# Cross entropy on one core: the first 64 rows split into groups of 16 and 48

## The chip, the core and the metric

The kernel runs on one NeuronCore of a Trainium2 chip. The metric is the device time of one execution in microseconds. Times of a kernel are medians over several runs; the profile is one more execution, taken with the hardware profiler.

## What is computed

For each of 256 rows of 32,000 float32 logits the result is minus the log probability of the row's label:

```
log_probs = logits - np.max(logits, axis=-1, keepdims=True)
log_probs = log_probs - np.log(np.sum(np.exp(log_probs), axis=-1, keepdims=True))
return np.array([-log_probs[i, labels[i]] for i in range(batch)])
```

The kernel leaves the maximum out (the logits are standard normal draws) and computes, for a row x with label l, the logarithm of sum_j exp(x_j) times exp(-x_l). That is the same number. The input is 256 x 32,000 x 4 bytes = 32.77 MB, each byte is read once, and the output is 1 KB.

## The kernel before

**Groups and loads.** The rows are cut into groups of 64, 128, 32 and 32. A group of k rows is spread over all 128 partitions: each row takes q = 128/k neighbouring partitions, and each partition holds 32,000/q consecutive elements of one row (the list `flat`). A group is loaded in pieces of columns:

```
GROUPS = [64, 128, 32, 32]
LOADS = [
    [1024, 14976],
    [8896, 8192, 8320, 6592],
    [4736, 3264],
    [2496, 1824, 1344, 992, 736, 608],
]
```

The numbers are elements per partition, so the 14 loads have the numbers 0 to 13. Load 0 takes the first 1,024 elements of each partition's 16,000, load 1 the other 14,976. For a partition, every load is one consecutive run in DRAM; from one partition to the next, in loads 0 and 1, the run moves on by 16,000 x 4 = 64,000 bytes.

**Slots.** Loads 0 to 5 have a buffer each (slots 0 to 5). Load 6 reuses slot 2, load 7 slot 3, and loads 8 to 13 lie side by side in slot 1 as `x_tail`. The slot sizes are multiples of 64 elements, and slot 0 begins with 32 unused elements (`SKIP`), so that with the 128 bytes of constants ahead of them every slot's data begin at a multiple of 256 bytes in the partition. In loads 0 to 8 the runs in DRAM also begin at multiples of 256 bytes from the tensor's start, and are multiples of 256 bytes long. From load 9 on, sizes such as 1,824 elements are odd multiples of 128 bytes, and some of the runs begin, in DRAM and in the slot alike, 128 bytes past a multiple of 256.

**Order.** All loads are issued by SyncE (SP, line 206) in order of number. The first is moved ahead of the barrier at the program's start (`begin_first_load_before_barrier`); loads 1 to 5 follow at once. Load 6 is issued when VectorE is done with the data of load 2, load 7 when it is done with those of load 3, and the six loads of the tail after these; the last of them, load 13, shares a semaphore with load 5 and waits until that has landed.

**Steps.** `step(i)` works on load i. ScalarE (ACT) takes the exponential of the whole piece in place (line 215). For loads 0, 1, 12 and 13 ScalarE also sums along the row of the partition as it goes (`accum_out`). For loads 2 to 11 (`HALVED`) VectorE (DVE) adds the two halves of the piece and sums the result (line 294). TensorE multiplies the 128 partial sums by a 128 x k matrix `weights` (line 300), which adds up the partitions of a row in PSUM. For the first group, the two sums of loads 0 and 1 are added by a VectorE reduction (line 284) and multiplied once (line 285). The logarithm is taken by ScalarE (line 222): for the first group between the exponentials of loads 2 and 3, for the others at the end. A store from SP (line 318) ends the program. Sixteen matmuls without use (line 291) come before the last products.

**The weights.** `weights` is 0 where a partition doesn't belong to a row, and exp(-x_l) of the row where it does. Its 0/1 pattern `holds` is made by GpSimd (POOL) with two selections for each group (lines 261 and 265). The labels arrive by a DMA from ScalarE's queue (line 229), are spread over the partitions, and lead two indirect DMAs of GpSimd (line 250) to the 256 label logits `g_at`. At the end of step 1 (`GATHERED`) ScalarE takes their exponential (line 274), VectorE makes two diagonal matrices (line 276), TensorE spreads them (line 279), and VectorE multiplies by `holds` (line 282).

Of the kernel before, what the change touches and what calls it, by code (L numbers as in the profile page):

```python
# [2 lines left out]

# [6 lines left out]
P = 128  # L10
ROWS = 2
F32 = mybir.dt.float32
I32 = mybir.dt.int32
AF = mybir.ActivationFunctionType

GROUPS = [64, 128, 32, 32]

LOADS = [  # L20
    [1024, 14976],
    [8896, 8192, 8320, 6592],
    [4736, 3264],
    [2496, 1824, 1344, 992, 736, 608],
]
CHUNKS = [n for ns in LOADS for n in ns]
GROUP_OF = [g for g, ns in enumerate(LOADS) for _ in ns]

# [10 lines left out]
GATHERED = 1  # L39

HALVED = range(2, 12)
# [75 lines left out]
def kernel(  # L117
# [6 lines left out]
    nc = tc.nc  # L124
    nc.at_finalize(begin_first_load_before_barrier)
    nc.at_finalize(end_before_store_lands)
    B, C = logits.shape
    assert B == P * ROWS == sum(GROUPS)
    row_at = [sum(GROUPS[:g]) for g in range(len(GROUPS) + 1)]
    for k, ns in zip(GROUPS, LOADS):  # L130
        assert P % k == 0 and sum(ns) * P == k * C
    assert C % (P // min(GROUPS)) == 0


    flat = [
        logits[row_at[g]:row_at[g + 1], :].rearrange("k (q c) -> (k q) c", q=P // k)
        for g, k in enumerate(GROUPS)
    ]
    starts = [sum(ns[:j]) for ns in LOADS for j in range(len(ns))]
    first_of = [GROUP_OF.index(g) for g in range(len(GROUPS))]  # L140
    last_of = [first_of[g] + len(ns) - 1 for g, ns in enumerate(LOADS)]
    last = len(CHUNKS) - 1

    big = ctx.enter_context(tc.tile_pool(name="big", bufs=1))
    small = ctx.enter_context(tc.tile_pool(name="small", bufs=1))
    psum = ctx.enter_context(tc.tile_pool(name="psum", bufs=1, space=bass.MemoryType.PSUM))

    width = {}
    for i, s in enumerate(SLOTS):
        width[s] = max(width.get(s, 0), CHUNKS[i])  # L150
    width[TAIL_SLOT] = max(width[TAIL_SLOT], sum(CHUNKS[TAIL:]))


    place = []
    for i, s in enumerate(SLOTS):
        skip = SKIP if s == 0 else 0
        t = big.tile([P, skip + width[s]], F32, name=f"x{i}", tag=f"slot{s}")
        place.append(t[:, skip:skip + CHUNKS[i]])
    assert all(width[s] % 64 == 0 for s in width)
    tail = big.tile([P, width[TAIL_SLOT]], F32, name="x_tail", tag=f"slot{TAIL_SLOT}")  # L160
    for i in range(TAIL, last + 1):
        at = sum(CHUNKS[TAIL:i])
        place.append(tail[:, at:at + CHUNKS[i]])


    assert HALVED[0] == last_of[0] + 1 and HALVED[-1] == last - 2
    assert all(CHUNKS[i] % 2 == 0 for i in HALVED)
    parts = small.tile([P, len(LOADS[0])], F32, name="parts")
    row_0 = small.tile([P, 1], F32, name="row_0")
    near = {i: small.tile([P, 1], F32, name=f"near{i}") for i in range(HALVED[0], last + 1)}  # L170
    res = small.tile([1, B], F32, name="res")
    ident = small.tile([P, P], F32, name="ident")
    ones = small.tile([P, P], F32, name="ones")
    diag = [small.tile([P, P], F32, name=f"diag{r}") for r in range(ROWS)]

    holds = small.tile([P, B], F32, name="holds")
    weights = small.tile([P, B], F32, name="weights")


    bank = [psum.tile([P, 512], F32, name=f"bank{b}") for b in range(5)]  # L180
    lane = []
    for g, k in enumerate(GROUPS):
        b = 0 if g == 0 else 2 if g == len(GROUPS) - 1 else 1
        at = row_at[g] if b == 1 else 0
        lane.append(bank[b][0:1, at:at + k])
    mid = bank[1][0:1, row_at[1]:row_at[-2]]
    spread = bank[3][:, 0:B]

    warm, lbl_up = bank[4][0:1, 0:P], bank[4][:, 0:ROWS]
# [14 lines left out]
    def load(i):  # L204
        a = starts[i]
        nc.sync.dma_start(out=place[i], in_=flat[GROUP_OF[i]][:, a:a + CHUNKS[i]])  # L206

    def exps(i):
        if i in HALVED:
            acc = None  # L210
        elif i > last_of[0]:
            acc = near[i][:, :]
        else:
            acc = parts[:, i:i + 1]
        nc.scalar.activation(out=place[i], in_=place[i], func=AF.Exp, accum_out=acc)  # L215

    def weigh(g):

        return weights[:, row_at[g]:row_at[g + 1]]

    def logs(rows, sums):
        nc.scalar.activation(out=res[0:1, rows], in_=sums, func=AF.Ln)  # L222

    with tc.manual_schedule():
        first = len(set(SLOTS))
        for i in range(first):
            load(i)

        nc.scalar.dma_start(
            out=words[:, :], in_=bass.AP(tensor=lbl_words, offset=0, ap=[[2 * B, 1], [1, 2 * B]])  # L230
        )


        assert C <= 1 << 24
        nc.vector.memset(one[:, :], 1.0)
        nc.vector.memset(ones[:, :], 1.0)
        nc.vector.tensor_copy(out=lbl_row[:, :], in_=words[:, 0:2 * B:2])  # L237
        for r in range(ROWS):
            nc.tensor.matmul(  # L239
                lbl_up[:, r:r + 1], lbl_row[:, r * P:(r + 1) * P], one[:, :], start=True, stop=True  # L240
            )
        nc.vector.tensor_copy(out=lbl[:, :], in_=lbl_up)  # L242
        for r in range(ROWS):
            nc.gpsimd.iota(
                out=idx[:, r:r + 1], pattern=[[1, 1]], base=r * P * C, channel_multiplier=C
            )
        make_identity(nc, ident[:, :])
        nc.gpsimd.tensor_add(out=idx[:, :], in0=idx[:, :], in1=lbl[:, :])
        for r in range(ROWS):
            nc.gpsimd.indirect_dma_start(  # L250
                out=g_at[:, r:r + 1],
                out_offset=None,
                in_=logits[:, :],
                in_offset=bass.IndirectOffsetOnAxis(ap=idx[:, r:r + 1], axis=1),
            )
        nc.gpsimd.memset(holds[:, :], 1.0)
        for g, k in enumerate(GROUPS):
            q = P // k
            h = holds[:, row_at[g]:row_at[g + 1]]

            nc.gpsimd.affine_select(  # L261
                out=h, in_=h, pattern=[[-q, k]], base=0, channel_multiplier=1,
                compare_op=mybir.AluOpType.is_ge, fill=0.0,
            )
            nc.gpsimd.affine_select(  # L265
                out=h, in_=h, pattern=[[q, k]], base=q - 1, channel_multiplier=-1,
                compare_op=mybir.AluOpType.is_ge, fill=0.0,
            )

        def step(i):  # L270
            exps(i)
            g = GROUP_OF[i]
            if i == GATHERED:
                nc.scalar.activation(out=eg[:, :], in_=g_at[:, :], func=AF.Exp, scale=-1.0)  # L274
                for r in range(ROWS):
                    nc.vector.tensor_scalar_mul(diag[r][:, :], ident[:, :], eg[:, r:r + 1])  # L276

                for r in range(ROWS):
                    nc.tensor.matmul(  # L279
                        spread[:, r * P:(r + 1) * P], ones[:, :], diag[r][:, :], start=True, stop=True  # L280
                    )
                nc.vector.tensor_mul(out=weights[:, :], in0=holds[:, :], in1=spread)  # L282
            if i == last_of[0]:
                nc.vector.reduce_sum(out=row_0[:, :], in_=parts[:, :], axis=mybir.AxisListType.X)
                nc.tensor.matmul(lane[0], row_0[:, :], weigh(0), start=True, stop=True)
            if i == last_of[0] + 1:
                logs(slice(0, row_at[1]), lane[0])
            if i == WARM_FROM:
                col = place[i][:, CHUNKS[i] - 1:CHUNKS[i]]
                for _ in range(WARM):  # L290
                    nc.tensor.matmul(warm, col, diag[0][:, :], start=True, stop=True)  # L291
            if i in HALVED:
                half = CHUNKS[i] // 2
                nc.vector.scalar_tensor_tensor(  # L294
                    out=place[i][:, 0:half], in0=place[i][:, 0:half], scalar=1.0,
                    in1=place[i][:, half:CHUNKS[i]],
                    op0=mybir.AluOpType.mult, op1=mybir.AluOpType.add, accum_out=near[i][:, :],
                )
            if g:
                nc.tensor.matmul(  # L300
                    lane[g], near[i][:, :], weigh(g), start=i == first_of[g], stop=i == last_of[g]
                )


        assert GATHERED <= last_of[0]
        done = 0
        for i in range(first, last + 1):
            slot = SLOTS[i] if i < TAIL else TAIL_SLOT
            while done <= SLOTS[:first].index(slot):
                step(done)  # L310
                done += 1
            load(i)
        for i in range(done, last + 1):
            step(i)

        logs(slice(row_at[1], row_at[-2]), mid)
        logs(slice(row_at[-2], B), lane[-1])
        nc.sync.dma_start(
            out=out.rearrange("(a n) -> a n", a=2), in_=res[0:1, :].rearrange("o (a n) -> o a n", a=2)
        )  # L320
# [30 lines left out]
```

## Time and profile before

| | before |
|---|---|
| median of 5 runs | 83.41 us (82.5 to 84.42) |
| the profiled execution's own time | 82.56 us |
| its span, first to last instruction | 80.9 us |
| ScalarE busy | 57.4 us, 71% |
| VectorE busy | 27.6 us, 34% |
| TensorE busy | 11.0 us, 14% |
| GpSimd busy | 5.2 us, 6% |
| read from HBM | 32.77 MB, 405 GB/s over the span |
| granted TensorE clock | 1.00 |

The share of busy time is a mean over stages. Where a stage waits is read from the idle time ahead of an instruction and what ended it. The execution with the profiler took 82.56 us, of which 80.9 us are span and 1.66 us lie around it; it is near the fastest of the five other runs.

### The profile page before, as it was taken

The page shows a single profiled execution, that of the slowest core. Times are in us where ns is not written, and L with a number is a line of the kernel's source. Part 1 is how long each engine was busy: PE and PEld are TensorE (multiplying, and loading weights), DVE is VectorE, ACT ScalarE, POOL GpSimd, SP SyncE. Part 2 cuts the span into 40 slices and gives each one's busy share as a digit, 9 for nine tenths or more (in the row PEclk, how much of TensorE's full clock was granted, in tenths as well). Part 3 has the DMA queues.
Part 4 walks back from the last instruction along what each step waited for, and adds up shares of the span by engine and source line. Part 5 has one row for each costly group of instructions (what it writes and reads, how often), then busy time and mean ns, then how long its engine had stood idle before and what let it go on. Part 6 is the DMA issues. An engine that isn't in the chain of part 4 may idle for free.

```text
span 80.9 us, 261 instructions
## 1 busy us (share of the span) xinstructions
PE 11.0 (14%) x66; PEld 6.2 (8%) x66; DVE 27.6 (34%) x28; ACT 57.4 (71%) x23; POOL 5.2 (6%) x20
## 2 busy tenths in 40 slices
PE   0130000000000000061000020020000201159931
PEld 0130000000000000040000000000000000036710
DVE  1100000000000000030039908930099198898870
ACT  6230000000499999999999991599979999999993
POOL 4038810000000000000000000000000000000000
PEclk9999999999999999999999999999999999999999
DMA  4999999579969799899898997999899999999930
GB/s 119 614 474 474 474 444 415 237 326 474 545 299 563 317 528 389 389 518 405 372 526 362 428 510 319 456 456 469 379 440 412 409 419 420 430 416 409 417 146 1
DMA packets 2084, 32.77 MB, mean 405 GB/s; under 512 B 290, under 2 KB 291, under 8 KB 1060
## 3 DMA queue, kind: packets, MB, share of 16 engines
q1 hardware_dynamic: 2018, 32.77, 94.9%
q0 software_dynamic: 64, 0.00, 0.1%
q10 hardware_dynamic: 2, 0.00, 0.0%
HBM read 32.77 MB, written 0.00 MB: 405 GB/s over the span
## 4 chain that ended last, share of the span: by engine, by line
DMA 61%; ACT 34%; SPq 1%; another core or an unknown queue 1%; issue 1%; PE 0%
DMA x<-in_logits_dram 61%; ACT x L215 24%; ACT x_tail L215 9%; SPq L206 1%; PE bank L300 0%; ACT res L222 0%
## 5 line engine op out<-in xcount | busy, mean ns | idle before, releaser
L215 ACT ACTIVATE x<-x 128x1024 f32<-128x1024 f32 (+7 forms) x8 | 48.1, 6030 | 21.4 <-DMA x<-in_logits_dram 21.4
L294 DVE SCALAR_TENSOR_TENSOR x<-x 128x4448 f32<-128x4448 f32 (+5 forms) x6 | 21.8, 3631 | 15.3 <-ACT x L215 15.3
L276 DVE TENSOR_SCALAR diag<-ident,eg 128x128 f32<-128x128 f32 x2 | 0.5, 284 | 29.4 <-ACT eg L274 29.4
L300 PE MATMUL bank<-weights,near 128*1 128x32 f32 (+1 forms) x24 | 3.7, 263 | 34.1 <-DVE x L294 32.3
L215 ACT ACTIVATE x_tail<-x_tail 128x2496 f32<-128x2496 f32 (+5 forms) x6 | 7.5, 1302 | 0.0
L279 PE MATMUL bank<-diag,ones 128*128 128x128 f32 x4 | 1.2, 461 | 30.0 <-DVE diag L276 30.0
L291 PE MATMUL bank<-diag,x 128*1 128x128 f32 x32 | 5.0, 333 | 0.0
L294 DVE SCALAR_TENSOR_TENSOR x_tail<-x_tail 128x1248 f32<-128x1248 f32 (+3 forms) x4 | 4.1, 1025 | 0.6 <-ACT x_tail L215 0.3
L300 PEld LDWEIGHTS bank<-weights,near 128*1 128x1 f32 x24 | 1.0, 82 | 36.8 <-DVE x L294 34.6
L291 PEld LDWEIGHTS bank<-diag,x 128*1 128x1 f32 x32 | 3.2, 102 | 1.6
L279 PEld LDWEIGHTS bank<-diag,ones 128*128 128x128 f32 x4 | 0.9, 324 | 30.1 <-DVE diag L276 30.1
L250 POOL DMA_INDIRECT g_at<-in_logits_dram,idx x2 | 2.1, 1031 | 0.6 <-issue 0.3
L198 ACT ACT_TABLE_LOAD x1 | 1.3, 1283 | 0.8 <-PEq L335 0.8
L239 PE MATMUL bank<-one,lbl_row 1*128 1x1 f32 x4 | 1.0, 352 | 3.8 <-DVE lbl_row L237 3.8
L239 PEld LDWEIGHTS bank<-one,lbl_row 1*128 1x128 f32 x4 | 0.9, 317 | 3.8 <-DVE lbl_row L237 3.8
L237 DVE CAST lbl_row<-words 1x256 f32<-1x256 int32 x1 | 0.3, 282 | 2.3 <-DMA words<-in_labels_dram 2.3
L265 POOL TENSOR_SCALAR_AFFINE_SELECT holds<-holds 128x32 f32<-128x32 f32 (+2 forms) x4 | 1.0, 238 | 0.3
L261 POOL TENSOR_SCALAR_AFFINE_SELECT holds<-holds 128x32 f32<-128x32 f32 (+2 forms) x4 | 1.0, 238 | 0.1
L282 DVE TENSOR_TENSOR weights<-holds,bank 128x256 f32<-128x256 f32 x1 | 0.4, 422 | 1.2 <-PE bank L279 1.2
L222 ACT ACTIVATE res<-bank 1x64 f32<-1x64 f32 (+2 forms) x3 | 0.7, 219 | 0.1
L242 DVE CAST lbl<-bank 128x2 int32<-128x2 f32 x1 | 0.2, 159 | 1.1 <-PE bank L239 1.1
L294 DVE DVE_READ_ACCUMULATOR x<-x 128x1 f32 x6 | 0.5, 82 | 0.0
(18 smaller groups left out, 3.7 us busy)
## 6 DMA issues: line engine op xcount, KB each, us to landing
x<-in_logits_dram SPq DMA_DIRECT2D x1, 7488.0 KB, 20.6
x<-in_logits_dram SPq DMA_DIRECT2D x1, 4448.0 KB, 30.7
x<-in_logits_dram SPq DMA_DIRECT2D x1, 4160.0 KB, 49.3
x<-in_logits_dram SPq DMA_DIRECT2D x1, 4096.0 KB, 39.9
x<-in_logits_dram SPq DMA_DIRECT2D x1, 3296.0 KB, 56.4
x<-in_logits_dram SPq DMA_DIRECT2D x1, 2368.0 KB
x<-in_logits_dram SPq DMA_DIRECT2D x1, 1632.0 KB, 15.3
x_tail<-in_logits_dram SPq DMA_DIRECT2D x1, 1248.0 KB
```

Of the source, the lines that this page charges most:

```text
L198: nc.scalar.preload_act_table_set("natural_log_exp_and_others")
L206: nc.sync.dma_start(out=place[i], in_=flat[GROUP_OF[i]][:, a:a + CHUNKS[i]])
L215: nc.scalar.activation(out=place[i], in_=place[i], func=AF.Exp, accum_out=acc)
L222: nc.scalar.activation(out=res[0:1, rows], in_=sums, func=AF.Ln)
L239: nc.tensor.matmul(lbl_up[:, r:r + 1], lbl_row[:, r * P:(r + 1) * P], one[:, :], start=True, stop=True)
L250: nc.gpsimd.indirect_dma_start(out=g_at[:, r:r + 1], out_offset=None, in_=logits[:, :], in_offset=bass.IndirectOffsetOnAxis(ap=idx[:, r:r ...
L261: nc.gpsimd.affine_select(out=h, in_=h, pattern=[[-q, k]], base=0, channel_multiplier=1, compare_op=mybir.AluOpType.is_ge, fill=0.0,)
L265: nc.gpsimd.affine_select(out=h, in_=h, pattern=[[q, k]], base=q - 1, channel_multiplier=-1, compare_op=mybir.AluOpType.is_ge, fill=0.0,)
L279: nc.tensor.matmul(spread[:, r * P:(r + 1) * P], ones[:, :], diag[r][:, :], start=True, stop=True)
L291: nc.tensor.matmul(warm, col, diag[0][:, :], start=True, stop=True)
L294: nc.vector.scalar_tensor_tensor(out=place[i][:, 0:half], in0=place[i][:, 0:half], scalar=1.0, in1=place[i][:, half:CHUNKS[i]], op0=mybir. ...
L300: nc.tensor.matmul(lane[g], near[i][:, :], weigh(g), start=i == first_of[g], stop=i == last_of[g])
```

## The change

The first group of 64 rows becomes two groups, of 16 and of 48 rows. The partitions of a group now simply divide the group's consecutive bytes by 128. For 16 rows this gives 4,000 elements each, an eighth of a row, and load 0 takes all of them: the 128 runs lie end to end in DRAM, 2.05 MB in one stretch. For 48 rows it gives 12,000 elements each. That is three eighths of a row, so a row can end inside a partition's run, but only at a multiple of 4,000: load 1 has three parts of 4,000 elements in each partition, and each part belongs to one row. Loads 2 to 13 are as before, with their numbers.

In DRAM the runs of load 0 are now 16,000 bytes long and 16,000 apart, and those of load 1 are 48,000 bytes long and 48,000 apart; these are odd multiples of 128 bytes, so the runs of every second partition begin 128 bytes past a multiple of 256. In the slots they begin at multiples of 256 still.

ScalarE takes the exponential of load 1 in three instructions, each with its sum. The reduction of line 284 goes; TensorE makes one product for load 0 and three for load 1, all into one PSUM bank. `holds` and `weights` get a column for each row and part, 352 instead of 256. GpSimd makes two more selections, and VectorE multiplies by `holds` in seven instructions, since the columns of the three parts use the same 48 columns of the spread label terms.

```
-GROUPS = [64, 128, 32, 32]
+GROUPS = [16, 48, 128, 32, 32]
 LOADS = [
-    [1024, 14976],
+    [4000],
+    [12000],
     [8896, 8192, 8320, 6592],
...
+EARLY = 1
...
+    span = [P // math.gcd(k, P) for k in GROUPS]
+    parts = [k // math.gcd(k, P) for k in GROUPS]
...
     flat = [
-        logits[row_at[g]:row_at[g + 1], :].rearrange("k (q c) -> (k q) c", q=P // k)
-        for g, k in enumerate(GROUPS)
+        logits[row_at[g]:row_at[g + 1], :].rearrange("k c -> (k c)").rearrange("(p n) -> p n", p=P)
+        for g in range(len(GROUPS))
     ]
...
-        width[s] = max(width.get(s, 0), CHUNKS[i])
+        width[s] = max(width.get(s, 0), -(-CHUNKS[i] // 64) * 64)
...
     def exps(i):
-        if i in HALVED:
-            acc = None
-        elif i > last_of[0]:
-            acc = near[i][:, :]
-        else:
-            acc = parts[:, i:i + 1]
-        nc.scalar.activation(out=place[i], in_=place[i], func=AF.Exp, accum_out=acc)
+        m = parts[GROUP_OF[i]]
+        n = CHUNKS[i] // m
+        for j in range(m):
+            x = place[i][:, j * n:(j + 1) * n]
+            nc.scalar.activation(
+                out=x, in_=x, func=AF.Exp, accum_out=None if i in HALVED else near[i][:, j:j + 1]
+            )
...
+    def products(i):
+        g = GROUP_OF[i]
+        for j in range(parts[g]):
+            nc.tensor.matmul(
+                lane[g], near[i][:, j:j + 1], weigh(g, j),
+                start=i == first_of[g] and j == 0, stop=i == last_of[g] and j == parts[g] - 1,
+            )
...
         for g, (k, n, m) in enumerate(zip(GROUPS, span, parts)):
             h = holds[:, cols_at[g]:cols_at[g + 1]].rearrange("p (m k) -> p m k", m=m)
             nc.gpsimd.affine_select(
-                out=h, in_=h, pattern=[[-q, k]], base=0, channel_multiplier=1,
+                out=h, in_=h, pattern=[[1, m], [-n, k]], base=0, channel_multiplier=m,
...
-                nc.vector.tensor_mul(out=weights[:, :], in0=holds[:, :], in1=spread)
-            if i == last_of[0]:
-                nc.vector.reduce_sum(out=row_0[:, :], in_=parts[:, :], axis=mybir.AxisListType.X)
-                nc.tensor.matmul(lane[0], row_0[:, :], weigh(0), start=True, stop=True)
+                for g, k in enumerate(GROUPS):
+                    for j in range(parts[g]):
+                        at = cols_at[g] + j * k
+                        nc.vector.tensor_mul(
+                            out=weigh(g, j), in0=holds[:, at:at + k],
+                            in1=spread[:, row_at[g]:row_at[g + 1]],
+                        )
+                for before in range(i):
+                    products(before)
...
-            if g:
-                nc.tensor.matmul(
-                    lane[g], near[i][:, :], weigh(g), start=i == first_of[g], stop=i == last_of[g]
-                )
+            if i >= GATHERED:
+                products(i)
```

More of the change, by code (lines that the diff above doesn't have):

```diff
@@ L1 @@
 import dataclasses
+import math
 from contextlib import ExitStack
@@ L129 @@
     row_at = [sum(GROUPS[:g]) for g in range(len(GROUPS) + 1)]
-    for k, ns in zip(GROUPS, LOADS):
-        assert P % k == 0 and sum(ns) * P == k * C
-    assert C % (P // min(GROUPS)) == 0
+    span = [P // math.gcd(k, P) for k in GROUPS]
+    parts = [k // math.gcd(k, P) for k in GROUPS]
+    for k, ns, n, m in zip(GROUPS, LOADS, span, parts):
+        assert sum(ns) * P == k * C and C % n == 0
+        assert m == 1 or len(ns) == 1
     flat = [
-        logits[row_at[g]:row_at[g + 1], :].rearrange("k (q c) -> (k q) c", q=P // k)
-        for g, k in enumerate(GROUPS)
+        logits[row_at[g]:row_at[g + 1], :].rearrange("k c -> (k c)").rearrange("(p n) -> p n", p=P)
+        for g in range(len(GROUPS))
     ]
@@ L163 @@
         place.append(tail[:, at:at + CHUNKS[i]])
-    assert HALVED[0] == last_of[0] + 1 and HALVED[-1] == last - 2
+    assert HALVED[0] == last_of[EARLY] + 1 and HALVED[-1] == last - 2
     assert all(CHUNKS[i] % 2 == 0 for i in HALVED)
-    parts = small.tile([P, len(LOADS[0])], F32, name="parts")
-    row_0 = small.tile([P, 1], F32, name="row_0")
-    near = {i: small.tile([P, 1], F32, name=f"near{i}") for i in range(HALVED[0], last + 1)}
+    near = [
+        small.tile([P, parts[GROUP_OF[i]]], F32, name=f"near{i}") for i in range(last + 1)
+    ]
     res = small.tile([1, B], F32, name="res")
@@ L174 @@
     diag = [small.tile([P, P], F32, name=f"diag{r}") for r in range(ROWS)]
-    holds = small.tile([P, B], F32, name="holds")
-    weights = small.tile([P, B], F32, name="weights")
+    cols_at = [sum(m * k for m, k in zip(parts[:g], GROUPS)) for g in range(len(GROUPS) + 1)]
+    holds = small.tile([P, cols_at[-1]], F32, name="holds")
+    weights = small.tile([P, cols_at[-1]], F32, name="weights")
     bank = [psum.tile([P, 512], F32, name=f"bank{b}") for b in range(5)]
@@ L182 @@
     for g, k in enumerate(GROUPS):
-        b = 0 if g == 0 else 2 if g == len(GROUPS) - 1 else 1
-        at = row_at[g] if b == 1 else 0
+        b = 0 if g <= EARLY else 2 if g == len(GROUPS) - 1 else 1
+        at = 0 if b == 2 else row_at[g]
         lane.append(bank[b][0:1, at:at + k])
-    mid = bank[1][0:1, row_at[1]:row_at[-2]]
+    soon = bank[0][0:1, 0:row_at[EARLY + 1]]
+    mid = bank[1][0:1, row_at[EARLY + 1]:row_at[-2]]
     spread = bank[3][:, 0:B]
@@ L208, in exps, with weigh @@
     def exps(i):
-        if i in HALVED:
-            acc = None
-        elif i > last_of[0]:
-            acc = near[i][:, :]
-        else:
-            acc = parts[:, i:i + 1]
-        nc.scalar.activation(out=place[i], in_=place[i], func=AF.Exp, accum_out=acc)
-    def weigh(g):
-        return weights[:, row_at[g]:row_at[g + 1]]
+        m = parts[GROUP_OF[i]]
[5 more added lines that the diff above has]
+            )
+    def weigh(g, j):
+        at = cols_at[g] + j * GROUPS[g]
+        return weights[:, at:at + GROUPS[g]]
+    def products(i):
[5 more added lines that the diff above has]
+            )
     def logs(rows, sums):
@@ L256 @@
         nc.gpsimd.memset(holds[:, :], 1.0)
-        for g, k in enumerate(GROUPS):
-            q = P // k
-            h = holds[:, row_at[g]:row_at[g + 1]]
+        for g, (k, n, m) in enumerate(zip(GROUPS, span, parts)):
+            h = holds[:, cols_at[g]:cols_at[g + 1]].rearrange("p (m k) -> p m k", m=m)
             nc.gpsimd.affine_select(
-                out=h, in_=h, pattern=[[-q, k]], base=0, channel_multiplier=1,
+                out=h, in_=h, pattern=[[1, m], [-n, k]], base=0, channel_multiplier=m,
                 compare_op=mybir.AluOpType.is_ge, fill=0.0,
@@ L265 @@
             nc.gpsimd.affine_select(
-                out=h, in_=h, pattern=[[q, k]], base=q - 1, channel_multiplier=-1,
+                out=h, in_=h, pattern=[[-1, m], [n, k]], base=n - 1, channel_multiplier=-m,
                 compare_op=mybir.AluOpType.is_ge, fill=0.0,
@@ L271, in step @@
             exps(i)
-            g = GROUP_OF[i]
             if i == GATHERED:
@@ L281, in step @@
                     )
-                nc.vector.tensor_mul(out=weights[:, :], in0=holds[:, :], in1=spread)
-            if i == last_of[0]:
-                nc.vector.reduce_sum(out=row_0[:, :], in_=parts[:, :], axis=mybir.AxisListType.X)
-                nc.tensor.matmul(lane[0], row_0[:, :], weigh(0), start=True, stop=True)
-            if i == last_of[0] + 1:
-                logs(slice(0, row_at[1]), lane[0])
+                for g, k in enumerate(GROUPS):
[7 more added lines that the diff above has]
+                    products(before)
+            if i == last_of[EARLY] + 1:
+                logs(slice(0, row_at[EARLY + 1]), soon)
             if i == WARM_FROM:
@@ L298, in step @@
                 )
-            if g:
-                nc.tensor.matmul(
-                    lane[g], near[i][:, :], weigh(g), start=i == first_of[g], stop=i == last_of[g]
-                )
-        assert GATHERED <= last_of[0]
+            if i >= GATHERED:
+                products(i)
+        assert GATHERED <= last_of[EARLY]
         done = 0
@@ L314 @@
             step(i)
-        logs(slice(row_at[1], row_at[-2]), mid)
+        logs(slice(row_at[EARLY + 1], row_at[-2]), mid)
         logs(slice(row_at[-2], B), lane[-1])
```

## The prediction

> **What bounds the kernel now.** I read the chain of waits that ended last first, then the DMA issues with their times to landing, then the timeline of ScalarE, then the windows. The chain, pieces in order of time (start us, length us, what):
>
> ```profile
> 2.12 49.27 DMA x<-in_logits_dram
> ...
> 51.41 7.14 ACT x L215
> 58.55 0.61 another core or an unknown queue
> ...
> 59.18 5.61 ACT x L215
> ...
> 71.80 7.46 ACT x_tail L215 x8
> ```
>
> The DMA stream carries the first 51.4 us. Then ScalarE works on load 4, waits 0.6 us more (for load 5, which lands at 59.16), and runs to the end without idling. The DMA issues give KB and us from issue to landing:
>
> ```profile
> x<-in_logits_dram SPq DMA_DIRECT2D x1, 7488.0 KB, 20.6
> x<-in_logits_dram SPq DMA_DIRECT2D x1, 4448.0 KB, 30.7
> x<-in_logits_dram SPq DMA_DIRECT2D x1, 4160.0 KB, 49.3
> x<-in_logits_dram SPq DMA_DIRECT2D x1, 4096.0 KB, 39.9
> x<-in_logits_dram SPq DMA_DIRECT2D x1, 3296.0 KB, 56.4
> ...
> x<-in_logits_dram SPq DMA_DIRECT2D x1, 512.0 KB, 3.5
> ```
>
> With the issue times in the timeline (load 0 at 0, load 1 at 0.8, load 2 at 1.18, load 3 at 1.66, load 4 at 2.12, load 5 at 2.78), loads 0 to 5 land at 3.50, 21.42, 31.91, 41.58, 51.39 and 59.16. Load 2 moves 4.55 MB in 10.49 us, 434 GB/s; loads 3, 4 and 5 give 434 each. Load 1 gives 7.67 MB in 17.92 us, 428. The last load lands at 78.34, and its exponential starts at 78.46, straight after the one before. So **the stream of loads, full from beginning to end, sets every date**, and ScalarE follows with almost no slack at the end. Loads 2 to 13 are not touched: the change counts only by the time at which the stream is done with loads 0 and 1, which have the same 8.19 MB before and after.
>
> ScalarE and VectorE at the seam, from the timeline (start us, us, engine):
>
> ```profile
> 3.52 1.06 ACT L215 ACTIVATE x<-x 128x1024 f32<-128x1024 f32 x1 [1.44 <-DMA x<-in_logits_dram]
> ...
> 21.44 12.68 ACT L215 ACTIVATE x<-x 128x14976 f32<-128x14976 f32 x1 [16.77 <-DMA x<-in_logits_dram]
> ...
> 34.12 0.19 ACT L274 ACTIVATE eg<-g_at 128x2 f32<-128x2 f32 x1
> 34.22 7.60 ACT L215 ACTIVATE x<-x 128x8896 f32<-128x8896 f32 x1
> ...
> 41.83 7.01 ACT L215 ACTIVATE x<-x 128x8192 f32<-128x8192 f32 x1
> ...
> 51.41 7.14 ACT L215 ACTIVATE x<-x 128x8320 f32<-128x8320 f32 x1 [2.57 <-DMA x<-in_logits_dram]
> ```
>
> ScalarE idles 16.8 us before load 1, is just behind load 3 (landed 41.58, started 41.83), and idles again 2.57 us before load 4. What is won or lost ahead of that by less than 2.57 us doesn't reach the end.
>
> **The stream at its start.** The trace keeps start, duration and size of each DMA packet. Each partition's run is one packet, 8 to an engine and load, on 16 engines. From load 2 on they hardly vary: 35,584 bytes take 1,316 ns, 7,296 bytes 276 ns, 2,432 bytes 98 ns, so a packet costs 8 ns + 0.03677 ns a byte. At the start they do vary. The first packet begins at 1.02 us; the sixteen first ones of 4,096 bytes take 211 to 692 ns, where the rule gives 159; all 128 have a mean of 203. The engines turn to load 1 between 2.65 and 3.16, and its packets of 59,904 bytes have a mean of 2,223 ns against 2,210 by the rule. The slowest engine ends load 1 at 21.01. Without any loss, packets following each other as they do in load 2, it would end at 1.02 + 8 x (0.159 + 2.210) = 19.97. The start-up costs the slowest engine **1.04 us** (0.70 in the mean, where the engines end at 20.67), and since the engines keep their distance through the following loads (20.44 to 21.01 at the start of load 2, 58.27 to 58.83 at that of load 6), the end inherits most of it.
>
> **The parts of the change.**
>
> *Packets of loads 0 and 1.* By the rule 16,000 bytes take 596 ns and 48,000 bytes 1,773. Sum: 8 x (0.596 + 1.773) = 18.95 us, the same as 8 x (0.159 + 2.210) = 18.95. Number and bytes of packets stay, so full rate gives 0.
>
> *The start-up loss.* Each engine's first 2.05 us of work were 8 short packets, 64,000 bytes apart; now the engine is in its fourth long packet by then. No row shows the start with long packets, so bounds: if all of the loss goes, -1.04 us; if it comes as now, 0; if every one of an engine's 16 packets lost what the first ones lose now in the mean (0.22 us), 3.5 us in place of the packets' present 0.45 (0.35 in load 0, 0.10 in load 1), +3.1. The nearest row is load 1: also long packets, right after the start, with 13 ns too much each. So I keep the late starts (1.02 to 1.33) and the latency of the first packet (mean 0.22, worst 0.53), and let the loss of the seven later ones (0.35 - 0.22 = 0.13 in the mean, more for the slowest) go: **-0.3 us**.
>
> *Misaligned runs.* Every second run of loads 0 and 1 starts 128 bytes past a multiple of 256 in DRAM but on one in SBUF. An engine has 4 such partitions of its 8: 4 x (0.596 + 1.773) = 9.5 us of its work. Lower bound 0: packets of load 10 (5,376 bytes, 128 past on both sides) take 206 ns, load 9's (7,296 bytes, an odd multiple of 128) 276, both on the rule; and the labels' 2,048 bytes, which go to an SBUF address 192 past a multiple of 256, take 81 ns, by the rule 83. Upper bound: as slow as the first packets were, mean 380 ns for 159, 2.4 times: +13 us. The rows nearest to it are those of the same offset: **0**. The Trainium skill's page "DMA: Bandwidth & Descriptors", section "How a descriptor splits into AXI transactions", speaks against the change: a run that doesn't start at a multiple of 256 bytes fetches bytes that it doesn't use, here 128 for each odd packet. As an estimate by that page it is 8 x 128 bytes an engine, at this trace's 0.03677 ns a byte 0.04 us, and the forecast would be -0.26 instead of -0.3.
>
> *ScalarE.* An exponential with its sum takes 0.8333 ns an element and 203 ns (1,056 for 1,024; 12,683 for 14,976). Load 0 needs 3.54 us instead of 1.06, in the 16.8 us idle before load 1. Load 1 needs 3 x 3.54 = 10.61 us instead of 12.68: -2.07. The label exponential is ready at 32.05, load 2 begins at 32.15 (landed at 31.91) and hands over at 32.15 + 7.61 = 39.76; then load 3 is waited for until 41.58 (+0.02), 0.23 earlier than now, and load 4 until 51.39 as before. All 2.07 us are swallowed by waits for loads. Without the wait for load 4, 0.23 would reach the end.
>
> *Weights and products.* VectorE's one multiply of 256 columns (422 ns) becomes seven. Between the 128x2 cast from PSUM (159 ns) and the 256 columns lies 1.04 ns a column: 176 + 3 x 209 + 292 + 2 x 190 = 1.48 us, +1.05; the reduction (0.15) goes. Four pairs of matmuls for one pair of 0.37: +1.1 at most. GpSimd has two more selections, by its rows 0.21 to 0.3 each, and a pattern 96 columns wider, in all some 0.6 us at 10 us into the run, needed at 34. From the label exponential: diagonals at 32.35, multiplies 34.03 to 35.5, products by 37. The logarithm that needs them stands on ScalarE after load 2's exponential, at 39.7; VectorE's next work is there at 39.8. Cost 0, slack 2.7 us; with that gone there is still the 1.8 us wait for load 3 behind.
>
> *SP and the other queues.* Load 6 waits for VectorE's halves of load 2: 39.8 + 4.87 = 44.7 instead of 46.68. Load 7 waits for those of load 3: 53.1 instead of 53.34; the tail follows, with load 13 at 59.17 as before. Load 5's packets end at 58.8, so all come in time: 0. The labels' packet may wait behind a packet of 0.6 us; the gathers landed at 14.73 and 19.21 and are needed at 32: 0.
>
> **Sum**: -0.3 us on the profile's 82.56, 82.26. That execution lies 0.85 below the median, and the steady packets leave hardly any room for such a spread, so the start, or what lies around the span, is where runs differ. Against the median: 83.41 - 0.3 = **83.1 us**. A measurement of this kernel tells about 1% (0.83 us) from no change.
>
> **Rivals.**
> 1. *The bytes decide; nothing moves*: 83.4. For it: equal sums, steady packets. The change needn't do what it says either: one stretch in DRAM is still read as 16 runs at once.
> 2. *The whole start-up loss goes*: 83.41 - 1.04 = 82.4; and if the slower runs have more of it, 82.0. For it: the loss sits in load 0, which is what changes. Against: late starts and first latency belong to any first packet.
> 3. *Slower: the misaligned half of loads 0 and 1 runs below full rate.* It is decided from 9% (0.83 of 9.5 us); at 15% +1.4 us, 84.8. For it: no row has source and destination off by different amounts at length, and the kernel pads its slots with care. Against: the labels' packet, but that is 2 KB.
>
> **How the numbers follow.** Forecast 0.36, rival 1 0.17, rival 2 0.22, rival 3 0.2, and 0.05 for a slower start (up to its bound of +3.1). The forecast reaches from 82.4 to 83.3 and gives 0.06 to faster; with rival 2 that is 0.28, slower 0.25, within 1% 0.47. The range takes in rivals 1 to 3 at their usual prices, 82.0 to 84.8; the far ends (+3.1 and +13) and a still larger gain stay out with some 2 in 10.
>
> **What would show it.** Right: load 1's packets of about 1,773 ns, load 1 landing near 21.1, loads 2 to 5 again 434 GB/s, ScalarE idle some 1.8 us before load 3 and 2.8 before load 4. Wrong: odd packets longer than even ones (rival 3), or load 1 landing at 20.5 (rival 2) or 21.4 (rival 1).

## The result, and the profile after

| | before | after |
|---|---|---|
| median | 83.05 us (75 runs, 82.49 to 85.31) | 83.37 us (38 runs, 83.12 to 83.59) |
| ratio after to before | | 1.005 (1.0034 to 1.0065) |
| the profiled execution's own time | 82.56 us | 83.43 us |
| its span | 80.9 us | 81.8 us |
| load 1 landed at | 21.42 us | 22.30 us |

The changed kernel is slower by half a per cent; 83.1 us and a gain of 0.3 had been forecast. That 83.37 lies only 0.3 us from 83.1 is luck: the forecast started from 83.41, the median of five runs of the kernel before, and over 75 runs that median is 83.05. The changed kernel's runs lie closer together than those of the kernel before. The ratio leaves out executions far above a kernel's fastest; the medians don't.

The chain of waits that ended last, of the kernel after (start us, us, what), has the same pieces as before:

```profile
2.43 49.84 DMA x<-in_logits_dram
...
52.30 7.14 ACT x L222
59.43 0.61 another core or an unknown queue
...
60.06 5.62 ACT x L222
...
72.69 7.46 ACT x_tail L222 x8
```

Everything from load 4 on is as long as it was and 0.9 us later: 52.30 for 51.41, 60.06 for 59.18, 72.69 for 71.80. The DMA issues of the kernel after (KB, us from issue to landing):

```profile
x<-in_logits_dram SPq DMA_DIRECT2D x1, 6000.0 KB, 21.5
x<-in_logits_dram SPq DMA_DIRECT2D x1, 4448.0 KB, 31.6
...
x<-in_logits_dram SPq DMA_DIRECT2D x1, 2000.0 KB, 8.1
```

Issued at 0.8, load 1 lands at 22.30; load 2 follows 10.49 us later, as before. So the whole 0.88 us is lost before load 1 lands, and nothing after it. ScalarE's timeline after (start us, us, and in brackets the idle time ahead and what ended it):

```profile
8.07 3.54 ACT L222 ACTIVATE x<-x 128x4000 f32<-128x4000 f32 x1 [5.99 <-DMA x<-in_logits_dram]
...
22.32 3.54 ACT L222 ACTIVATE x<-x 128x4000 f32<-128x4000 f32 x1 [10.61 <-DMA x<-in_logits_dram]
...
32.89 0.19 ACT L290 ACTIVATE eg<-g_at 128x2 f32<-128x2 f32 x1
...
42.47 7.03 ACT L222 ACTIVATE x<-x 128x8192 f32<-128x8192 f32 x1 [1.78 <-DMA x<-in_logits_dram]
...
52.30 7.14 ACT L222 ACTIVATE x<-x 128x8320 f32<-128x8320 f32 x1 [2.80 <-DMA x<-in_logits_dram]
```

Load 1's exponentials take 32.89 - 22.32 = 10.57 us instead of 12.68, and the waits for loads 3 and 4 (1.78 and 2.80 us) swallow the difference.

Where the 0.88 us go is seen in the DMA packets, whose start, duration and size the trace keeps. The steady rule is the prediction's: 8 ns + 0.03677 ns a byte. "Loss" means the time over this rule, and "first" are the sixteen packets of a load that start earliest. The trace doesn't name a packet's engine. Where packets are short, a few of these sixteen are second packets of an engine that is already done with its first (the prediction's own count, a mean of 380 ns and 0.22 us over the rule, is 389 and 0.23 by this one).

| kernel | load 0: run, distance (bytes) | loss, first of load 0: mean, worst (ns) | load 1 begins (us) | loss, first of load 1: mean, worst (ns) | load 1 landed (us) | that execution (us) |
|---|---|---|---|---|---|---|
| before | 4,096, 64,000 | 231, 533 | 2.65 to 3.16 | 35, 182 | 21.42 | 82.56 |
| after | 16,000, 16,000 | 833, 1,836 | 6.41 to 7.72 | 0, 0 | 22.30 | 83.43 |

After, the sixteen first packets take 1,430 ns in the mean where the steady rule gives 596, and one engine's takes 2,432. Followed from packet to packet (each starts where another ends, 8 to an engine and load), that engine is the last one to the end of load 1 (21.91, mean of all 21.20; before 21.01 and 20.67). From the second packets on the loss is small in the mean (185 ns, then 14, 4, 2 and 0), though one of them, begun at 1.89 us, still loses 1,064; load 1 has none.

### The profile page after: what moved, and what is told of

The parts are those of the page before. It is cut to its first block, busy times and chain, and to the rows that moved or that the text cites. A ratio compares the mean times of both kernels' runs of the same rounds, so it can differ in the third digit from the quotient of the medians.

```text
span 81.8 us, 290 instructions
## 1 busy us (share of the span) xinstructions
PE 12.6 (15%) x72; PEld 7.1 (9%) x72; DVE 28.0 (34%) x33; ACT 57.9 (71%) x27; POOL 5.8 (7%) x22
## 4 chain that ended last, share of the span: by engine, by line
DMA 61%; ACT 33%; SPq 2%; another core or an unknown queue 1%; issue 1%; PE 0%
DMA x<-in_logits_dram 61%; ACT x L222 24%; ACT x_tail L222 9%; SPq L215 2%; PE bank L234 0%; ACT res L240 0%
## 5 line engine op out<-in xcount | busy, mean ns | idle before, releaser
L222 ACT ACTIVATE x<-x 128x4000 f32<-128x4000 f32 (+6 forms) x10 | 48.5, 4863 | 21.8 <-DMA x<-in_logits_dram 21.8
L234 PE MATMUL bank<-weights,near 128*1 128x32 f32 (+3 forms) x32 | 4.3, 259 | 35.3 <-DVE x L315 34.3
L312 PE MATMUL bank<-diag,x 128*1 128x128 f32 x32 | 6.4, 390 | 0.0
L234 PEld LDWEIGHTS bank<-weights,near 128*1 128x1 f32 x32 | 1.5, 83 | 38.2 <-DVE x L315 36.5
L312 PEld LDWEIGHTS bank<-diag,x 128*1 128x1 f32 x32 | 3.7, 118 | 2.4
L301 DVE TENSOR_TENSOR weights<-holds,bank 128x48 f32<-128x48 f32 (+3 forms) x7 | 0.9, 200 | 1.2 <-PE bank L295 1.2
L282 POOL TENSOR_SCALAR_AFFINE_SELECT holds<-holds 128x32 f32<-128x32 f32 (+3 forms) x5 | 1.2, 247 | 0.3
L278 POOL TENSOR_SCALAR_AFFINE_SELECT holds<-holds 128x32 f32<-128x32 f32 (+3 forms) x5 | 1.2, 249 | 0.1
L222 ACT ACTIVATION_READ_ACCUMULATOR x<-x 128x1 f32 x4 | 0.7, 186 | 0.0
```

The lines of the kernel that those rows point to most:

```text
L222: nc.scalar.activation(out=x, in_=x, func=AF.Exp, accum_out=None if i in HALVED else near[i][:, j:j + 1])
L234: nc.tensor.matmul(lane[g], near[i][:, j:j + 1], weigh(g, j), start=i == first_of[g] and j == 0, stop=i == last_of[g] and j == parts[g] - 1,)
L278: nc.gpsimd.affine_select(out=h, in_=h, pattern=[[1, m], [-n, k]], base=0, channel_multiplier=m, compare_op=mybir.AluOpType.is_ge, fill=0.0,)
L282: nc.gpsimd.affine_select(out=h, in_=h, pattern=[[-1, m], [n, k]], base=n - 1, channel_multiplier=-m, compare_op=mybir.AluOpType.is_ge, fi ...
L301: nc.vector.tensor_mul(out=weigh(g, j), in0=holds[:, at:at + k], in1=spread[:, row_at[g]:row_at[g + 1]],)
```

## The experiments

Three theories. **L**: an engine's first packet runs at some 11 GB/s over its whole length, so longer first packets lose more. **C**: the place of load 0 costs, one stretch of 2 MB instead of runs 64,000 bytes apart. **M**: the runs that begin 128 bytes past a multiple of 256 cost. A fourth, **T**, comes with the shorter first runs. "Beside it" means the kernel before in the same group of runs on the same chip. Each packet figure comes from one profiled execution of its kernel.

**Longer first runs at the old distance.** Of the kernel before:

```
-    [1024, 14976],
+    [4032, 11968],
```

> The kernel before with load 0 of 4,032 elements instead of 1,024 (load 1 has 11,968): runs of 16,128 bytes, 64,000 bytes apart as before, all at multiples of 256. Theory L (an engine's first packet runs at about 11 GB/s over its whole length, 4,096 bytes in 389 ns before and 16,000 in 1,430 after, wherever it lies): first packets of about 1,440 ns in the mean, load 1 landing near 22.3, time as the changed kernel, 83.4. Rival C (it is the one stretch of 2 MB that is slow to open): first packets lose some 0.23 us each as before, about 830 ns, load 1 lands near 21.4 and the time is that of before, 83.05.

First packets: 1,280 ns, 679 over the rule, near L's 1,440; worst 1,070 over. But load 1 landed at 21.53, and the time is 82.60 us (82.51 to 82.70) against 82.62 beside it, ratio 0.9985 (0.9969 to 1.000). L is right about the first packets and wrong about the time: the mean engine loses 0.45 us more there than before, but it loses nothing in load 1, and the last engine ends load 1 at 21.12 against 21.01.

**Short runs in one stretch.** Of the changed kernel:

```
-GROUPS = [16, 48, 128, 32, 32]
+GROUPS = [4, 60, 128, 32, 32]
...
-    [4000],
-    [12000],
+    [1000],
+    [15000],
```

> The changed kernel with groups of 4 and 60 rows: load 0 has 1,000 elements in each partition, 128 runs of 4,000 bytes end to end, one stretch of 0.5 MB; load 1 has 15 parts of 1,000 elements. Theory L: first packets of some 380 ns as before, load 1 lands near 21.4. Rival C: the first packets lose as much as after, 0.83 us each, or more, since all 16 engines start within 64 KB of each other; load 1 lands at 22 or later. ScalarE needs 15 x 1.04 = 15.5 us for load 1 instead of 10.6, which the waits for loads 4 and 5 should still hide.

First packets 421 ns, 266 over the rule, near the 231 of the kernel before: here the length of the packet rules, as L says. But load 1, which begins at 2.67 to 3.33 us, loses 268 ns in its first packets in the mean and 1,065 in the worst, and lands at 22.37. Time 83.60 us, ratio 1.0091 (1.0055 to 1.0127). The loss can move from load 0 into load 1.

**Runs of 8,000 bytes in one stretch.** The same with `[8, 56, 128, 32, 32]`, `[2000]` and `[14000]`.

> The changed kernel with groups of 8 and 56 rows: runs of 8,000 bytes in load 0, one stretch of 1 MB, and 7 parts of 2,000 elements in load 1. Theory L: first packets of about 715 ns, 0.41 us over the steady 302, load 1 landing near 21.7, time between the two kernels, 83.2. Rival C: as after, load 1 at 22.3 and 83.4.

First packets 780 ns, 478 over (L: 410); load 1 at 21.66 (L: 21.7, C: 22.3); 82.80 us, 82.62 beside it, ratio 1.0002 (0.9977 to 1.0028). Near L, and not C: one stretch of 1 MB in runs of 8,000 bytes costs 0.18 us by the medians and nothing by the ratio.

**Shorter first runs.** Of the kernel before, `[256, 15744]`.

> The kernel before with load 0 of 256 elements instead of 1,024: runs of 1,024 bytes, 64,000 apart. Theory L, if the slow packet is the very first whatever its length: 1,024 bytes at 11 GB/s take about 95 to 150 ns, the loss of the first packets shrinks from 0.23 to below 0.1 us, load 1 lands up to 0.2 earlier, time 82.9. Rival T (an engine runs slowly for its first microsecond or its first 4 KB, not for its first packet): the loss moves into the next packets, up to the first one of load 1, which then loses up to several us if it is slow over all of its 62,976 bytes, load 1 landing anywhere from 21.4 to 24.

Load 0's first packets lose 57 ns. The engines begin load 1 at 1.79 to 2.43 us, and its first packets, of 62,976 bytes, lose 848 ns in the mean and 1,309 in the worst; its second ones 41. Load 1 lands at 22.54; 83.85 us, ratio 1.0137 (1.0112 to 1.0162). So it is rival T of the expectation: a long packet that begins in the first microseconds is slow, be it an engine's first or its ninth. ScalarE's timeline of this kernel shows it, 1.1 us later than before:

```profile
2.15 0.42 ACT L215 ACTIVATE x<-x 128x256 f32<-128x256 f32 x1
...
22.57 13.32 ACT L215 ACTIVATE x<-x 128x15744 f32<-128x15744 f32 x1 [19.90 <-DMA x<-in_logits_dram]
```

**The place of load 0 alone.** Four runs on one chip: the changed kernel again; load 0 with its 16,000 bytes at the old distance; load 1 with its 48,000 bytes at the old distance; load 0 at the old distance plus 128 bytes. The edit of the second one; the third and fourth have `{1: (4000, 16000)}` and `{0: (0, 16032)}`. A load that is moved reads other logits, so the results of its rows are other sums; number, size and order of the packets stay.

```
+RUNS = {0: (0, 16000)}
...
+        src = flat[GROUP_OF[i]][:, a:a + CHUNKS[i]]
+        if i in RUNS:
+            at, step = RUNS[i]
+            src = bass.AP(tensor=logits.tensor, offset=at, ap=[[step, P], [1, CHUNKS[i]]])
```

> The changed kernel itself, on the same chip as the next three, as their measure. Both theories: first packets of about 1,430 ns, the worst near 2,400, load 1 landing at 22.2 to 22.4, 83.1 to 83.6 us.

> The changed kernel with load 0 read from runs of 16,000 bytes that lie 64,000 apart instead of end to end (it then holds other logits than the first 16 rows, so the first 16 results are other sums; size, order and everything else stay). Theory C (the single stretch slows the worst engine's first packets): the worst first packet falls from 2,432 to about 1,700 ns, load 1 lands near 21.5, 82.6 us. Rival P (the new pieces and lengths, or load 1, make the difference): as the changed kernel, 22.3 and 83.4. Rival M (the odd multiples of 128 bytes): 64,000 is a multiple of 256, so as theory C here.

> The changed kernel with load 0 in its one stretch, but load 1 read from runs of 48,000 bytes that lie 64,000 apart, as in the kernel before (load 1 holds other logits than rows 16 to 63, so those results are other sums). Theory C, with the place of load 0: no change against the changed kernel, 22.3 and 83.4. Rival P with load 1 as its cause: back to 21.5 and 82.6.

> As the run with load 0 at the old pitch, but the runs are 64,128 bytes apart, so every second one begins 128 past a multiple of 256 as in the changed kernel (the first 16 results are other sums). Theory C: as with 64,000, load 1 lands near 21.5, 82.6 us. Rival M (misaligned runs cost): the second packets lose some 0.18 us in the mean and up to 1 us as in the changed kernel, load 1 lands 0.2 to 0.8 later, 82.8 to 83.4 us.

| | loss, first of load 0: mean, worst (ns) | load 1 landed (us) | median us (range) |
|---|---|---|---|
| changed kernel | 888, 1,857 | 22.36 | 83.38 (83.31 to 83.51) |
| load 0 at 64,000 | 498, 803 | 21.53 | 82.65 (82.50 to 83.17) |
| load 1 at 64,000 | 781, 1,811 | 22.31 | 83.37 (83.16 to 83.51) |
| load 0 at 64,128 | 524, 942 | 21.56 | 82.66 (82.33 to 83.15) |

C holds for runs of 16,000 bytes (with 8,000 it didn't), and M falls: the place of load 0 alone is worth 83.38 - 82.65 = 0.73 us, and the ranges don't touch. Load 1's place, the three parts, the two groups and the 128 bytes are worth nothing that shows. ScalarE's timeline of the changed kernel in this group:

```profile
8.09 3.54 ACT L222 ACTIVATE x<-x 128x4000 f32<-128x4000 f32 x1 [6.01 <-DMA x<-in_logits_dram]
...
22.39 3.54 ACT L222 ACTIVATE x<-x 128x4000 f32<-128x4000 f32 x1 [10.67 <-DMA x<-in_logits_dram]
```

and with load 0 at 64,000:

```profile
7.23 3.54 ACT L229 ACTIVATE x<-x 128x4000 f32<-128x4000 f32 x1 [5.15 <-DMA x<-in_logits_dram]
...
21.55 3.54 ACT L229 ACTIVATE x<-x 128x4000 f32<-128x4000 f32 x1 [10.69 <-DMA x<-in_logits_dram]
```

Load 0 is there 0.86 us earlier (7.23 for 8.09), and load 1 0.84 (21.55 for 22.39).

**Other distances.** `{0: (0, 32000)}` and `{0: (0, 8000)}`, and the grouping before with `[4032, 11968]` once more.

> The changed kernel with the runs of load 0 128,000 bytes apart (one in each of 128 rows; the first 16 results are other sums). If the first packets are slow because they lie close together, the loss goes on falling with the distance: mean loss of the first packets below the 0.50 us that 64,000 gave, worst first packet at 1,400 ns or less, load 1 landing at 21.5 or earlier, 82.4 to 82.6 us. Rival (only a stretch without gaps is slow, or the loss is a fixed price of any first packet once there is some distance): 0.5 us and 21.5 as with 64,000, 82.65 us.

> The same with the runs 32,000 bytes apart, twice their length (the first 16 results are other sums). Distance theory: between 16,000 (0.83 to 0.89 us over the rule, worst about 2,400 ns, landing 22.3) and 64,000 (0.50 us, 1,400 ns, 21.5): some 0.65 us, worst near 1,900 ns, landing near 21.9, 83.0 us. Rival (only the stretch without gaps): as 64,000, 21.5 and 82.65.

> The kernel before with load 0 of 4,032 elements and load 1 of 11,968, once more and with more rounds, as a candidate that computes the whole result. If what spreads the times of the kernel before sits in its short first packets, this one keeps within 82.5 to 82.8 and is 0.2 to 0.4% faster by the medians; otherwise no difference, ratio 1.000 within 0.002.

At 128,000 bytes the first packets lose 556 ns (worst 1,186), load 1 lands at 21.67, 82.53 us (4 runs, 82.43 to 82.77): nothing to be seen beyond the 82.65 that 64,000 gave on another chip. At 32,000: 596 ns, worst 1,416, landing 22.16, 83.01 us (82.83 to 83.26), slower than 128,000 on the same chip and between 64,000 and end to end, as the distance theory had it. The old grouping with 4,032 elements gave 82.66 us (82.46 to 83.12) while the kernel before took 83.68 beside it (82.81 to 84.99): ratio **0.9912** (0.9877 to 0.9948). In the first group of runs the same two had been equal. So something slows the kernel before in some groups of runs, and not the kernel with longer first runs.

**What slows the kernel before.** Five more profiles of it, and `[2048, 13952]` as a step between.

> The kernel before itself, looked at again. Its times spread from 82.4 to 85.3 while the kernels with long first runs keep within some 0.6 us, and its one profile is of 82.56, near the lower end. If the spread sits in the start of the stream, a look at 83.3 or more shows load 1 landing later than 21.42 by the same amount, by slow packets in loads 0 and 1, and every later distance between landings as before. If it sits elsewhere, load 1 lands at 21.4 and a later load is late, or the time around the span grows.

> The kernel before with load 0 of 2,048 elements and load 1 of 13,952: runs of 8,192 bytes, 64,000 apart. If the spread belongs to first packets that are too short, this lies between the kernel before and the one with 4,032: up to 83.5 in some runs, some slow first packets in load 1. If 8 KB is long enough, 82.5 to 82.7 in all runs, load 1 landing near 21.4.

The three profiled executions of the kernel before in this group took 82.58 to 82.60 us, load 1 at 21.42 to 21.49. Their first packets of load 0 lost 401, 497 and 324 ns in the mean, more than the 231 of the first profile, and yet load 1 landed at most 0.07 us later than there. The kernel with 2,048: 82.60 (82.54 to 82.75), 82.63 beside it, ratio 0.9989 (0.9979 to 0.9999). In the next group:

> The kernel before in another group of runs, where its times may be spread as in its 75 runs. If this look is above 83.0 and the excess sits in the start, load 1 lands later than 21.42 by it; if not, load 1 is at 21.4 and a later distance between landings is longer. At 82.6 it tells nothing new.

> The same kernel beside it once more: load 1 later than 21.42 by what the time is over 82.56 if the excess sits in the start, at 21.4 if it sits elsewhere.

> The kernel before with 8 KB first runs again, beside the kernel before. If the longer first run makes the start steady, it stays at 82.5 to 82.75 whatever the kernel before does; if groups of runs differ for every kernel alike, it moves with the kernel before.

Here the two profiled executions of the kernel before took 84.13 and 82.89 us. ScalarE's timeline of the first of them:

```profile
3.38 1.06 ACT L215 ACTIVATE x<-x 128x1024 f32<-128x1024 f32 x1 [1.30 <-DMA x<-in_logits_dram]
...
22.98 12.68 ACT L215 ACTIVATE x<-x 128x14976 f32<-128x14976 f32 x1 [18.45 <-DMA x<-in_logits_dram]
```

and of the second:

```profile
3.52 1.06 ACT L215 ACTIVATE x<-x 128x1024 f32<-128x1024 f32 x1 [1.44 <-DMA x<-in_logits_dram]
...
21.80 12.68 ACT L215 ACTIVATE x<-x 128x14976 f32<-128x14976 f32 x1 [17.14 <-DMA x<-in_logits_dram]
```

Load 0 is as early as ever, and load 1 late by 1.54 and 0.36 us (landed 22.96 and 21.78); the times are late by 1.57 and 0.33. The packets name the place: the first packets of load 1, begun at 2.6 to 3.6 us, lose 175 ns in the mean and 1,425 in the worst (107 and 590 in the second), where the four fast executions had 19 to 35 and 111 to 336. The kernel with 2,048 elements begins load 1 at 3.82 to 4.38, loses 16 ns there (worst 142), and took 82.40 us (82.36 to 82.45), 83.17 beside it: ratio **0.990** (0.9825 to 0.9975), four runs of it. Its timeline:

```profile
4.74 1.91 ACT L215 ACTIVATE x<-x 128x2048 f32<-128x2048 f32 x1 [2.66 <-DMA x<-in_logits_dram]
...
21.32 11.83 ACT L215 ACTIVATE x<-x 128x13952 f32<-128x13952 f32 x1 [14.58 <-DMA x<-in_logits_dram]
```

Both kernels with the old grouping and a longer load 0 compute the whole result. They are as fast as the kernel before at its best and about 1% faster where it isn't.

Over the executions cited here, the time less the landing of load 1 is nearly constant: before 82.56 - 21.42 = 61.14; after 83.43 - 22.30 = 61.13; 256 elements in load 0 83.67 - 22.54 = 61.13; the late execution of the kernel before 84.13 - 22.96 = 61.17.

## Why the prediction was wrong

**The bound was right.** The stream of loads sets every date, and only the landing of load 1 counts: the sums just made show it.

**The step that failed is the start-up loss.** It kept "the latency of the first packet (mean 0.22, worst 0.53)" as a fixed price and let 0.3 us of the rest go. The first packets' price isn't fixed: in the changed kernel it is 0.83 us in the mean and 1.84 in the worst. Two things raise it.

- The length of the packet, though less than in proportion: at the distance of 64,000 the first packets lost 57 ns on 1,024 bytes, 231 to 497 on 4,096 (six executions), 316 and 504 on 8,192, and 498 to 679 on 16,000 and 16,128 (three executions).
- The distance, for runs of 16,000 bytes: 498 ns at 64,000, 596 at 32,000, 781 to 888 end to end. The worst engine, which sets the landing, goes from 803 to 1,070 ns at 64,000 to 1,811 to 1,857.

Nor did the rest go: the seven later packets of load 0 lose 0.20 us an engine, where they lost 0.12; only load 1's 0.10 went. Together an engine loses 1.04 us in the mean instead of 0.45. So the mean end of load 1 is 0.53 us later (21.20 for 20.67), and the last engine, with the worst first packet, 0.90 (21.91 for 21.01). The forecast had -0.3 us for this term; against its own profile it measured +0.88. The bound of +3.1 contained it. The value was taken from load 1 of the kernel before, as the nearest row, and that was the wrong row: it began 1.6 us later, and the run with `[256, 15744]` shows that a load of nearly the same length is slow when it begins at 1.8 to 2.4 us.

**The longer packets alone would have been right for the time, by another way.** At the old distance the same lengths cost nothing (0.9985) or gain 1% (0.9912). They lose more in load 0, but load 1 then begins after 3.8 us and loses almost nothing. The prediction's doubt that runs differ at the start was right as far as it was seen: two executions show the whole excess in load 1. The change has this gain too; its runs keep within 0.5 us. It pays for it with 0.73 us for the stretch. In the two comparisons that ran both, the net is +0.5% (1.005 and 1.0046). Over the five groups of runs in the experiments, the medians of the kernel before lay at 82.62 to 83.68, so by an estimate across groups the net is between +0.9% and less than nothing.

**Misaligned runs: right, 0.** Of load 1's 128 packets 123 take 1,773 ns and none over 1,780, so odd and even are alike, and 64,128 bytes made no difference to 64,000 (82.66 for 82.65). The bytes that the page "DMA: Bandwidth & Descriptors" of the Trainium skill, section "How a descriptor splits into AXI transactions", has fetched in vain would be some 5 ns an odd packet by my estimate; no such difference shows in the 1,773.

**ScalarE: right.** -2.07 was forecast for load 1, 12.68 - 10.57 = 2.11 was measured; waits of 1.8 and 2.8 us, measured 1.78 and 2.80.

**Weights and products: right in their cost of 0**, too dear in their sizes. The timeline after:

```profile
34.86 0.91 DVE L301 TENSOR_TENSOR weights<-holds,bank 128x16 f32<-128x16 f32 x7 [1.19 <-PE bank L295]
...
35.18 0.78 PE L234 MATMUL bank<-weights,near 128*1 128x16 f32 x8 [0.42 <-DVE weights L301]
40.49 0.20 ACT L240 ACTIVATE res<-bank 1x64 f32<-1x64 f32 x1
```

Seven multiplies took 0.91 us together (1.48 forecast; each 171 to 279 ns, and they overlap), and the products were done at 35.96, 4.5 us ahead of the logarithm.

**SP and the queues: right in their cost, wrong in one size.** The labels' packet was to wait up to 0.6 us; VectorE's first use of the labels moved from 3.43 to 6.16 us. The gathers landed at 16.51 and 20.14 for 14.73 and 19.21, and are needed at 32.9.

**Rivals.** "Load 1 landing at 21.4" (nothing moves) and "20.5" (all of the loss goes) are both refuted by 22.30, as is the forecast's own 21.1; the misaligned half has no cost. What came was the "slower start", which had 0.05.

**What stays open.** Why a long packet that begins in the first microseconds is slow, and why the distance matters, isn't shown; nor why a stretch that costs 0.73 us with runs of 16,000 bytes costs so little with 8,000, which engine is the worst, or what makes the kernel before meet it in one group of runs and not in the next, on one chip too.

## What to carry to other kernels

This stream, full from beginning to end, was decided by its start and by its slowest engine. In such a stream, read the first sixteen packets and the last engine to leave the first loads, not only bytes and means. Here first runs of 8 to 16 KB, 64,000 bytes apart, were the steady choice; 1 KB runs let the big load begin too early, and one end-to-end stretch of 16,000-byte runs made load 1 land 0.8 to 0.9 us later. A single profile near the fast end of a spread hides what the spread is made of; take more profiles before forecasting a gain from it.

## What the hardware showed that I had not expected

First packets ran at 6 to 15 GB/s an engine in the mean (4,096 bytes in 389 to 656 ns, 8,000 in 780, 16,000 in 1,094 to 1,484) against 27 in the steady state. A packet of 62,976 bytes begun at 1.8 to 2.4 us took 3,172 ns in the mean instead of 2,324, with the engine's ninth place in line no help. The first packets of load 1, where they began after 3.8 us, were within 20 ns of the rule in the mean. When a long packet begins (with 256 elements in load 0, load 1 landed 1.1 us later) mattered as much as where its run lies (0.8 to 0.9).
